# The logits' second product in mixers A and B: 64 rows of the array, or 80 and 128 with zeros added

## The chip, the core and the metric

One core of a Trainium2 chip runs the whole kernel. The metric is the device time of one execution in microseconds (us), the median of three runs; lower is better.

## What is computed

One layer of a decoder over 1024 tokens of 1024 channels, all in float32. The input is normed and projected to the columns of three causal attention mixers and of the merge gates. Each mixer has 8 query heads of 64 channels, with normed queries and keys:

```python
# A: compressed blocks, selected blocks and a 256-key window, two key/value heads, three gated branches
logits = einsum('bgrqd,bgqkd->bgrqk', q, k_selected) * scale + bias;  p = softmax(where(valid, logits, -1e30))
logits = einsum('bgrnqd,bgnkd->bgrnqk', q, k_window) * scale + bias   # window 256
o = gate0 * o_cmp + gate1 * o_slc + gate2 * o_win
# B: window of 128 keys, two key/value heads, a learned sink per head in the softmax
# C: dense causal attention, eight key heads, a cumulative log forget gate added to the logits
x = x + (gates * einsum('btnm,nmd->btnd', branches, w_branch)).sum(2) @ w_out
x = x + conv_ffn(rms_norm(x, norm_ffn))
```

## The kernel before

**Split operands.** TensorE (PE) multiplies float32 data in a reduced form, so each operand is split into a high part and a low remainder, and a product is summed from the three larger partial products. Dense projections do that with three matmuls for each piece of 128 contracted rows (`mm3_steps`, lines 258 to 260, three groups in the trace: high by high, high by low, low by high).

**Logits.** A head has 64 channels, half of the array's 128 rows. `make_k` (line 581) builds from a key head two tiles of 128 rows and 1024 keys: U holds the high part twice, V the low part in rows 0 to 63; rows 64 up are free for extra rows. `make_q` (line 618) builds for 512 queries X, with the high part in rows 0 to 63 and the low part in rows 64 to 127, and where wanted Y, with the high part again and extra rows below. The logits of 128 queries against a bank of up to 512 keys are then two matmuls into one PSUM bank S (function `logits` in `unit`): line 676 multiplies X and U over 128 rows (high by high and low by high in one), and the second product adds high by low:

```python
nc.tensor.matmul(p, z["x"][:, z["qs"]], u[:, ks], start=True, stop=False)                              # 676
if kext is None:
    nc.tensor.matmul(p, z["x"][0:64, z["qs"]], v[0:64, ks], start=False, stop=True)                    # 678
else:
    nc.tensor.matmul(p, z["y"][0:64 + kext, z["qs"]], v[0:64 + kext, ks], start=False, stop=True)      # 680
```

The extra rows carry additive terms: mixer C puts its forget gates into 4 of them (68 rows), and mixer A's selected branch, for the later 512 queries (c = 1), a block pattern in V (a DMA on POOL's queue, line 1219) and the unseen blocks in Y (16 rows, 80 in all). The other logits need no extra rows and use line 678 over 64 rows: all of A's window branch, A's selected branch for the first 512 queries (c = 0), and all of mixer B. These are 64, 32 and 64 matmuls, 160 in all.

**A unit** (`unit`, line 655) is two such lots of logits. DVE adds the bias table and takes the row extreme on S (line 695, or 691 without a table), ACT takes the exponential (704), DVE the reciprocal of the sum (747), and POOL scales the probabilities p in place (753). Later PE transposes p (788), ACT and DVE split the transposes into high and low (795, 796), and PE multiplies them with the split values (811, 812) into O, which ACT and DVE fold (876, 877) and a DMA stores to scratch.

**Order.** Mixers C, A and B run in this order. PE's instructions stand in an order that the program itself writes: `Line.drive` takes steps from three streams (attention units; transposes and value products; the dense projections as filling) by a rough model of the queues. The other engines' queues are put in order by the framework's scheduler. So what PE does next is fixed: when an operand is late, everything behind it on PE waits. Mixer A's outputs are projected in `merge` (line 1340) while mixer B still runs; B's projection, the output projection and the MLP follow behind with nothing but dense matmuls on PE.

Of the kernel before, what the change touches and what calls it, by code (L numbers as in the profile page):

```python
# [37 lines left out]
# column offsets of the input projection  # L38
# [12 lines left out]
def _onehot(dist, valid, relative):  # L51
    """[33, n]: minus the one-hot of the bucket (less that of the last bucket), row 32 marks invalid."""
    n = dist.shape[0]
    oh = np.zeros((N_BUCKETS + 1, n), np.float32)
    cols = np.arange(n)
    b = _bucket(dist)
    oh[b, cols] -= 1.0
    if relative:
        oh[N_BUCKETS - 1, :] += 1.0
    oh[:, ~valid] = 0.0  # L60
    oh[N_BUCKETS, ~valid] = 1.0
    return oh
# [29 lines left out]
class Slots:  # L92
    """When each of n buffers is free, in the order of use; one that is taken counts as never free until it is put."""
# [14 lines left out]
class Line:  # L108
    """A rough model of the engines' queues, to put streams of work into one order of issue for TensorE."""
# [12 lines left out]
    def on(self, eng, ready, dur):  # L122
        """When an operation of an engine ends that takes the first gap in its queue."""
        t = max(ready, self.now) + self.HOP
        q = self.busy[eng]
        while q and q[0][1] < self.now:
            q.pop(0)
        k = 0
        while k < len(q) and q[k][0] < t + dur:
            t = max(t, q[k][1])  # L130
            k += 1
        q.insert(k, (t, t + dur))
        return t + dur

    def later(self, t, act, *args, tag=None):
        """Have act called at time t: a store queued before its data are there would hold up the loads behind it."""
        heapq.heappush(self.due, (t, next(self.count), tag, partial(act, *args)))
# [5 lines left out]
    def room(self, tag, bufs):  # L143
        """Before a tile of these bufs takes the place of one that is still to be stored."""
        while sum(z[2] == tag for z in self.due) >= bufs:
            self.settle(min(z[0] for z in self.due if z[2] == tag))

    def drive(self, *streams):
        """Streams by falling priority: generators that yield a function telling when their next step may issue."""
        at = [next(x, None) for x in streams]  # L150
        while any(at):
            self.settle(self.now)
            times = [NEVER if f is None else f() for f in at]
            if self.due and self.now < self.due[0][0] < min(times):
                self.now = self.due[0][0]
                continue
            k = next((q for q, t in enumerate(times) if t <= self.now), None)
            if k is None:
                k = min(range(len(at)), key=lambda q: times[q])
                assert times[k] < NEVER, "no stream can go on"  # L160
                self.now = times[k]
            at[k] = next(streams[k], None)
            if at[k] is None and k < 2 and not any(at[:2]):
                self.ended()
        self.settle(NEVER)


class Builder:
# [49 lines left out]
    def wload(self, pools, rows, c0, ncol, nk):  # L218
        """rows: DRAM AP [nk*128, cols]; list of (hi, lo) APs [128, ncol], one for each k piece."""
# [29 lines left out]
    def mm3_steps(self, out, pairs, last, there=None):  # L249
        """out += sum of (hi + lo).T @ (hi + lo) less lo.T @ lo, over pairs ((lhi, llo), (rhi, rlo))."""  # L250
# [66 lines left out]
    def rms_cols(self, pool, acc, rstd):  # L317
        """rstd [128, n] per token from acc [128, n * 128], the squares summed over the d tiles."""
# [9 lines left out]
    def bcast_cols(self, pool, col, dst):  # L328
        """dst [128, 512] = col [128, 4] laid along the free dim, on every partition."""
        nc = self.nc  # L330
        p = self.ps("O")
        for q in range(4):
            b = self.t(pool, [P, P], F32, "bc", 2)
            nc.vector.tensor_scalar(b, self.ones, col[:, q:q + 1], None, op0=ALU.mult)
            nc.tensor.matmul(p[:, q * P:(q + 1) * P], b, self.ident, start=True, stop=True)
        nc.scalar.copy(dst, p)

# [1 line left out]
    # chunk: (first column, columns, [(kind, from, to)]); n: normed heads, v: plain, g: branch gates, f: forget gates  # L339
# [12 lines left out]
    def first(self, xp, s0, wp, sp):  # L352
        """x, normed but for the factor of each token, split; beside it two chunks of the projection."""
# [43 lines left out]
    def tok_chunk(self, wp, sp, name, w=None, done=()):  # L397
        """Token-major columns of the projection to DRAM scratch; yields the PE time spent."""
# [57 lines left out]
    def gate_chunks(self, wp, sp, rbc):  # L456
        """tanh of half the merge gates, d-major, to DRAM scratch."""
# [39 lines left out]
    def lo_first(self, w, bs):  # L497
        """Both halves' products with x's low parts, which then are not needed any more."""
# [14 lines left out]
    def forget(self, sp):  # L513
        """Cumulative log forget gate, heads on partitions, split and laid out for the logits."""
        nc = self.nc
        # log_sigmoid(x) = min(x, 0) - log1p(e), e = exp(-|x|); log1p(e) = 2 atanh(e / (2 + e))
# [54 lines left out]
    def load_tok(self, ap_, tag, name, c0, n, t0, nt, bufs):  # L571
        """Columns of the projection, token-major; (tile, when it is there)."""
# [8 lines left out]
    def make_k(self, ap_, src, gcol):  # L581
        """src [128, 8, 64] token-major; U = [k_hi; k_hi], V = [k_lo; extra rows], [128, 1024] each."""
# [3 lines left out]
        v = self.t(ap_, [P, T], F32R, "V", 2)  # L586
        g = self.gain[0:64, gcol:gcol + 1]
# [17 lines left out]
    def make_v(self, ap_, src):  # L605
        """src [128, 8, 64]; VV [128, 8, 128] = [v_hi | v_lo]."""
# [10 lines left out]
    def make_q(self, ap_, qt, pair, gcol, want_y):  # L617
        """qt [128, 4, cols] token-major; X = [q_hi; q_lo], Y = [q_hi; extra rows], [128, 512] for two heads."""
# [11 lines left out]
        for h in range(2):  # L630
# [6 lines left out]
            if want_y:  # L637
                y = self.t(ap_, [P, 512], F32R, "Y", 4)
                nc.gpsimd.tensor_scalar(y[0:64, :], x[0:64, :].bitcast(F32), 1.0, 1.0, op0=ALU.mult, op1=ALU.mult)
# [9 lines left out]
    def unit(self, ap_, head, c_out, two, at, u, v, kext, span, vv, flags, done=None):  # L649
        """two: of each (query tile, x, y, near, first maximum, gate, sink); a query sees span key tiles.  # L650
        near(w): list of (c0, c1, table or None) for the last bank, covering all its columns [0, w)."""
# [19 lines left out]
        def logits(z, n, bank, base):  # L671
# [5 lines left out]
            if kext is None:  # L677
                nc.tensor.matmul(p, z["x"][0:64, z["qs"]], v[0:64, ks], start=False, stop=True)  # L678
# [78 lines left out]
    def pv_jobs(self, ap_, head, c_out, tiles, span, pts, vv, flags, done):  # L757
        """o[:, c_out:c_out + 256] += [v_hi | v_lo].T @ p.T for two lots of 128 queries, of the same query tile or of successive ones."""
# [67 lines left out]
    def t_stream(self, ap_):  # L826
        """Transposes and products with the values, some banks of the first ahead of the second."""
# [44 lines left out]
    def out_bank(self, ap_, o, n, h, t0, heads):  # L872
        """A bank's outputs, of heads from h on and 512 / heads queries from t0 on, to DRAM scratch."""
# [24 lines left out]
    def fox(self, ap_):  # L898
# [23 lines left out]
        def queries(h, c):  # L922
            """Of the heads h and h + 1."""
# [45 lines left out]
    def near_table(self, pool, m):  # L969
        """(tile, when it is there): [128 queries, 8 heads, 256 keys of the same and the previous tile, backwards]."""  # L970
# [7 lines left out]
    def last(tab, h, w):  # L978
        """The table's part for the last w keys."""
# [21 lines left out]
    def windows(self, tp, which):  # L1001
        """The compression windows of both groups, [positions of a pair, pair, 2 * 64 windows], split."""
# [33 lines left out]
    def compress(self, tp, wp, which, bh, bl):  # L1036
# [8 lines left out]
        # tanh form of gelu, twice its value  # L1045
# [93 lines left out]
    def select(self, ap_, e, r):  # L1139
        """BIG at the key blocks that a query does not see, [128, 4, 16]."""  # L1140
        nc = self.nc
        w5 = self.t(ap_, [P, 512], F32, "pcTl", 1)[:, 0:256].rearrange("p (a j) -> p a j", j=16)
        # key blocks 4 j - 1 to 4 j + 3; what stands before a head's first block is a zero (its neighbour's last one is
        # never valid)
# [17 lines left out]
    def cmp_jobs(self, ap_, heads, e, at, pair, g):  # L1162
        """The compressed branch's part of two heads' outputs, in two banks."""
# [35 lines left out]
    def mixer_a(self, ap_, tcm):  # L1199
# [5 lines left out]
        def queries(g, c, pair):  # L1205
            if pair == 0:
                nxt["qt"] = self.load_tok(ap_, "qt", f"aq{g}", 0, 256, c * 4, 4, 1)
            return (yield from self.make_q(ap_, nxt["qt"], pair, 0, c == 1))
# [3 lines left out]
        for g in range(2):  # L1212
# [4 lines left out]
            uw, vw, w_at = yield from self.make_k(ap_, kw, 1)  # L1217
# [6 lines left out]
            for c in range(2):  # L1224
                xy = first
                for pair in range(2):
# [22 lines left out]
                    for tp in range(2):  # L1249
# [25 lines left out]
                        for q in range(2):  # L1275
                            end = None
                            if q == 1:
# [3 lines left out]
                                                 16 if c == 1 else None, NT, vvs, (False, q == 1), done=end)  # L1281
# [3 lines left out]
    def mixer_b(self, ap_):  # L1285
# [5 lines left out]
        def keys(g):  # L1291
            kt = self.load_tok(ap_, "kt", "bkv", g * 64, 64, 0, NT, 2)
            vt = self.load_tok(ap_, "kt", "bkv", P + g * 64, 64, 0, NT, 2)
            u, v, there = yield from self.make_k(ap_, kt, 3)
# [44 lines left out]
    def merge(self, n, first, macc, mp, wps, sp):  # L1339
        """Add a branch's gates times projection to macc; split the sum at the end when mp is given."""  # L1340
# [47 lines left out]
    def out_proj(self, x1, wps, hp_, sp):  # L1388
        """Residual stream after the mixers, and its normed parts, by halves of the tokens."""
# [218 lines left out]
```

## Time and profile before

| | us |
|---|---|
| device time, median of 3 runs (2033.54 to 2034.82) | 2034.41 |
| span of the profiled execution, first to last instruction | 2033.2 |
| PE busy / its weight loads (PEld) | 2005.0 / 1699.0 |
| DVE / ACT / POOL busy | 1184.6 / 817.8 / 419.5 |

The profiled execution's own time is known by its span alone; the median of the runs lies 1.2 us above it, within the spread of the runs. "L678" in a row is line 678 of the kernel. In a list of PE's instructions in order of time the start counts: matmuls are pipelined, so the duration of one reaches into the next, and PE's busy time includes stretches in which the pipeline is not full. The step from one start to the next is what a matmul costs there. PEld is the load of the stationary operand (128 columns) ahead of each matmul, which can run while the matmul before it streams.

### The profile page before, as it was taken

What the parts mean: (1) busy time and instruction counts of PE and PEld (TensorE: products, weight loads), DVE (VectorE), ACT (ScalarE), POOL (GpSimd) and SP (SyncE); (2) the same over time, 40 slices, a digit from 0 to 9 for tenths busy, and PEclk for the clock granted to TensorE, in tenths of its full rate; (3) what the DMA queues carried; (4) which work ended last, traced back from release to release, by engine and by line L of the source; (5) the groups of instructions that cost most, each with busy time, mean ns of one, the idle gap of its engine ahead of it and who ended that gap; (6) DMA issues with size and microseconds to landing.
All of it is one profiled execution on the core that took longest, in us unless ns stands there. A gap on an engine that the chain in (4) does not pass through costs nothing.

```text
span 2033.2 us, 30629 instructions
## 1 busy us (share of the span) xinstructions
PE 2005.0 (99%) x11047; PEld 1699.0 (84%) x11047; DVE 1184.6 (58%) x2571; ACT 817.8 (40%) x1791; POOL 419.5 (21%) x582
## 2 busy tenths in 40 slices
PE   8999999999999999999999999999999999999999
PEld 8999999998788877888777888888888888888887
DVE  6746677766666666666777675564534434445333
ACT  4434566654545545355765233331221211212211
POOL 2224556544312213122121440000000000000000
PEclk9999999999999999999999999999999999999999
DMA  6434232322221221212434644221111120111102
GB/s 200 139 102 130 76 85 81 97 76 65 56 88 47 67 66 59 71 53 83 126 107 132 211 153 135 68 63 52 42 52 42 42 62 26 58 53 52 47 26 83
DMA packets 179562, 166.23 MB, mean 82 GB/s; under 512 B 41569, under 2 KB 157297, under 8 KB 179412
## 3 DMA queue, kind: packets, MB, share of 16 engines
q1 hardware_dynamic: 179348, 164.15, 27.4%
q8 instruction: 87, 1.43, 0.3%
q14 instruction: 63, 0.52, 0.1%
q0 software_dynamic: 64, 0.13, 0.0%
HBM read 126.20 MB, written 38.04 MB: 81 GB/s over the span
## 4 chain that ended last, share of the span: by engine, by line
PE 93%; DVE 3%; DMA 1%; issue 1%; ACT 1%; POOL 1%; SPq 0%; ACTq 0%; DVEq 0%; POOLq 0%
PE D L258 13%; PE D L259 13%; PE D L260 13%; PE S L259 7%; PE S L258 7%; PE S L260 7%; PE T L788 4%; PE T L260 4%; PE T L259 4%; PE T L258 4%; PE S L676 3%; PE O L811 3%; PE O L812 2%; PE S L678 2%; PE S L680 1%
## 5 line engine op out<-in xcount | busy, mean ns | idle before, releaser
L234 ACT CAST whi<-wraw 128x512 fp32r<-128x512 f32 (+2 forms) x308 | 189.4, 621 | 373.1 <-PE S L259 136.6
L235 DVE TENSOR_TENSOR wlo<-wraw,whi 128x512 fp32r<-128x512 f32 (+2 forms) x308 | 227.1, 743 | 98.8 <-ACT whi L234 94.4
L704 ACT ACTIVATE p<-S,mf 128x512 f32<-128x512 f32 (+3 forms) x320 | 174.4, 548 | 115.6 <-DVE mf L695 102.4
L796 DVE TENSOR_TENSOR pTl<-T,pTh 128x512 fp32r<-128x512 f32 (+2 forms) x248 | 151.0, 616 | 89.5 <-ACT pTh L795 87.3
L258 PE MATMUL D<-whi,xh 128*128 128x256 f32 (+2 forms) x680 | 200.5, 295 | 2.6 <-ACT whi L234 2.6
L259 PE MATMUL D<-wlo,xh 128*128 128x256 f32 (+2 forms) x680 | 193.1, 284 | 2.0 <-DVE wlo L235 2.0
L260 PE MATMUL D<-whi,xl 128*128 128x256 f32 (+2 forms) x680 | 192.6, 283 | 0.0
L795 ACT CAST pTh<-T 128x512 fp32r<-128x512 f32 (+2 forms) x248 | 128.3, 532 | 138.3 <-PE T L788 126.6
L259 PE MATMUL D<-xl,whi 128*128 128x512 f32 x464 | 183.2, 395 | 0.0
L753 POOL TENSOR_SCALAR p<-p,den,gates 128x384 f32<-128x384 f32 (+3 forms) x160 | 107.5, 685 | 326.3 <-DVE den L747 183.8
L258 PE MATMUL D<-xh,whi 128*128 128x512 f32 x368 | 155.8, 423 | 0.0
L260 PE MATMUL D<-xh,wlo 128*128 128x512 f32 x368 | 144.9, 394 | 0.0
L258 PE MATMUL S<-xl,whi 128*128 128x512 f32 x352 | 138.4, 394 | 0.0
L260 PE MATMUL S<-xl,wlo 128*128 128x512 f32 x352 | 138.4, 394 | 0.0
L788 PE MATMUL T<-c,p 128*128 128x128 f32 x864 | 130.5, 274 | 5.9 <-POOL p L753 3.7
L258 PEld LDWEIGHTS D<-whi,xh 128*128 128x128 f32 x680 | 129.3, 190 | 6.2 <-ACT whi L234 3.2
L259 PEld LDWEIGHTS D<-wlo,xh 128*128 128x128 f32 x680 | 129.5, 190 | 3.3 <-DVE wlo L235 2.4
L260 PEld LDWEIGHTS D<-whi,xl 128*128 128x128 f32 x680 | 129.1, 190 | 0.0
L811 PE MATMUL O<-pTh,VV 128*128 128x256 f32 x448 | 122.8, 297 | 1.3 <-DVE osum L877 1.3
L258 PE MATMUL D<-xl,whi 128*128 128x512 f32 x304 | 122.6, 403 | 0.0
L753 POOL TENSOR_SCALAR p<-p,den 128x256 f32<-128x256 f32 (+3 forms) x160 | 89.7, 577 | 147.9 <-DVE den L747 94.1
L260 PE MATMUL D<-xl,wlo 128*128 128x512 f32 x304 | 119.8, 394 | 0.0
(323 smaller groups left out, 4896.4 us busy)
## 6 DMA issues: line engine op xcount, KB each, us to landing
wraw<-w_in SPq DMA_DIRECT2D x96, 256.0 KB
s_gate<-stage SPq DMA_DIRECT2D x48, 256.0 KB
stage<-s_gate SPq DMA_DIRECT2D x48, 256.0 KB
wraw<-w_gate SPq DMA_DIRECT2D x44, 256.0 KB
wraw<-w_up SPq DMA_DIRECT2D x44, 256.0 KB
wraw<-w_down SPq DMA_DIRECT2D x44, 256.0 KB
wraw<-w_out SPq DMA_DIRECT2D x32, 256.0 KB
wraw<-w_branch SPq DMA_DIRECT2D x24, 256.0 KB
```

The source lines that it names most:

```text
L234: nc.scalar.copy(hi[:, :m, :ncol], raw[:, :m, :ncol])
L235: nc.vector.tensor_tensor(out=lo[:, :m, :ncol], in0=raw[:, :m, :ncol], in1=hi[:, :m, :ncol].bitcast(F32), op=ALU.subtract)
L258: nc.tensor.matmul(out, lh, rh, start=(k == 0), stop=False)
L259: nc.tensor.matmul(out, lh, rl, start=False, stop=False)
L260: nc.tensor.matmul(out, ll, rh, start=False, stop=(k == n - 1))
L676: nc.tensor.matmul(p, z["x"][:, z["qs"]], u[:, ks], start=True, stop=False)
L704: nc.scalar.activation(pt, z["tiles"][n][:, :w], AF.Exp, bias=z["m"], scale=-1.0, accum_out=den[:, n, q:q + 1])
L753: nc.gpsimd.tensor_scalar(pt, pt, d0[:, q:q + 1], 1.0 if gate is None else gate, op0=ALU.mult, op1=ALU.mult)
L788: nc.tensor.transpose(p[:, c0:c0 + P], z["t"][:, k:k + P], self.ident)
L795: nc.scalar.copy(ph[:, lo:hi], p[:, lo:hi])
L796: nc.vector.tensor_tensor(out=pl[:, lo:hi], in0=p[:, lo:hi], in1=ph[:, lo:hi].bitcast(F32), op=ALU.subtract)
L811: nc.tensor.matmul(ow, vv[:, kj, :], parts["h"][:, cs], start=(b_first and s == 0), stop=False)
```

## The change

The second product is issued over more rows, the added ones zero on one side. Line 678 now reads X and V over all 128 rows; for that `make_k` takes a flag `plain` that sets rows 64 to 127 of V to zero with POOL, used for A's window keys and for B's keys. The selected branch always takes the path of line 680 with 16 extra rows; for c = 0 `make_q` now makes Y too, and sets its 16 extra rows to zero with POOL. Comments and docstrings were removed as well, which shifts later line numbers by up to 5: 676 becomes 681, 678 becomes 683, 680 becomes 685, 639 becomes 644, 753 becomes 758; the new zeroing stands at lines 588 (V) and 643 (Y).

```diff
-    def make_k(self, ap_, src, gcol):
+    def make_k(self, ap_, src, gcol, plain=False):
...
         v = self.t(ap_, [P, T], F32R, "V", 2)
+        if plain:
+            nc.gpsimd.memset(v[64:128, :].bitcast(F32), 0.0)
...
-    def make_q(self, ap_, qt, pair, gcol, want_y):
+    def make_q(self, ap_, qt, pair, gcol, want_y, zeros=0):
...
                 y = self.t(ap_, [P, 512], F32R, "Y", 4)
+                if zeros:
+                    nc.gpsimd.memset(y[64:64 + zeros, :].bitcast(F32), 0.0)
                 nc.gpsimd.tensor_scalar(y[0:64, :], x[0:64, :].bitcast(F32), 1.0, 1.0, op0=ALU.mult, op1=ALU.mult)
...
             if kext is None:
-                nc.tensor.matmul(p, z["x"][0:64, z["qs"]], v[0:64, ks], start=False, stop=True)
+                nc.tensor.matmul(p, z["x"][:, z["qs"]], v[:, ks], start=False, stop=True)
...  mixer_a
-            return (yield from self.make_q(ap_, nxt["qt"], pair, 0, c == 1))
+            return (yield from self.make_q(ap_, nxt["qt"], pair, 0, True, 16 if c == 0 else 0))
...
-            uw, vw, w_at = yield from self.make_k(ap_, kw, 1)
+            uw, vw, w_at = yield from self.make_k(ap_, kw, 1, True)
...
-                                                 16 if c == 1 else None, NT, vvs, (False, q == 1), done=end)
+                                                 16, NT, vvs, (False, q == 1), done=end)
...  mixer_b
-            u, v, there = yield from self.make_k(ap_, kt, 3)
+            u, v, there = yield from self.make_k(ap_, kt, 3, True)
```

On PE no instruction changes its place; 32 second products read Y in place of X, and 128 read more rows. The first window units of mixer A, PE before (S is the logits' bank, D a dense projection that fills in):

```order
L812 MATMUL O_6196<-pTl_6436,VV_5558 128x256
L676 MATMUL S_6475<-U_6194,X_6184 128x256
L678 MATMUL S_6475<-V_6195,X_6184 128x256
L676 MATMUL S_6481<-U_6194,X_6187 128x256
L678 MATMUL S_6481<-V_6195,X_6187 128x256
L676 MATMUL S_6492<-U_6194,X_6184 128x256
L678 MATMUL S_6492<-V_6195,X_6184 128x256
L258 MATMUL D_6400<-whi_6162,xh_37_118 128x256
```

and of the change:

```order
L817 MATMUL O_6203<-pTl_6443,VV_5558 128x256
L681 MATMUL S_6482<-U_6200,X_6184 128x256
L683 MATMUL S_6482<-V_6201,X_6184 128x256
L681 MATMUL S_6488<-U_6200,X_6190 128x256
L683 MATMUL S_6488<-V_6201,X_6190 128x256
L681 MATMUL S_6499<-U_6200,X_6184 128x256
L683 MATMUL S_6499<-V_6201,X_6184 128x256
L258 MATMUL D_6407<-whi_6162,xh_37_118 128x256
```

The rows stand in the same order; only the tiles' numbers differ.

On POOL's queue 20 instructions are new: 4 of line 588, 8 of line 643 and 8 copies into Y (644). The end of mixer C and the start of A, POOL before (p is probabilities to be scaled, the last unit of mixer C; pTh and pTl the split transposes; sqh and rr belong to a projection's norm; blk is the block pattern):

```order
L753 TENSOR_SCALAR p_6036<-p_6036,den_5994 128x512
L753 TENSOR_SCALAR p_6038<-p_6038,den_5994 128x384
L753 TENSOR_SCALAR p_6092<-p_6092,den_5994 128x512
L753 TENSOR_SCALAR p_6094<-p_6094,den_5994 128x512
L428 TENSOR_TENSOR sqh_6145<-stage_6142 128x256
L802 MEMSET pTh_6210 128x128
L803 MEMSET pTl_6211 128x128
L433 TENSOR_TENSOR rr_6147<-rr_6147,mhalf_74 128x4
L599 TENSOR_SCALAR U_6194<-U_6194 64x512
L1219 DMA V_6266<-blk 16x1024
L599 TENSOR_SCALAR U_6194<-U_6194 64x512
```

and of the change:

```order
L1224 DMA V_6273<-blk 16x1024
L643 MEMSET Y_6558 16x512
L758 TENSOR_SCALAR p_6036<-p_6036,den_5994 128x512
L758 TENSOR_SCALAR p_6038<-p_6038,den_5994 128x384
L758 TENSOR_SCALAR p_6092<-p_6092,den_5994 128x512
L758 TENSOR_SCALAR p_6094<-p_6094,den_5994 128x512
L428 TENSOR_TENSOR sqh_6145<-stage_6142 128x256
L807 MEMSET pTh_6217 128x128
L808 MEMSET pTl_6218 128x128
L644 TENSOR_SCALAR Y_6187<-X_6184 64x512
L644 TENSOR_SCALAR Y_6193<-X_6190 64x512
L433 TENSOR_TENSOR rr_6147<-rr_6147,mhalf_74 128x4
```

The DMA of the block pattern and a zeroing of Y moved ahead of the scaling of mixer C's last unit, and two copies into Y stand behind it; the same move of the DMA occurs at the second group of mixer A.

## Rows read from the trace of the kernel before

**Rows 1.** The page: the span, TensorE's busy time with its share of the span and its instructions, and the chain of work that ended last, by engine.

```profile
span 2033.2 us, 30629 instructions
PE 2005.0 (99%) x11047; PEld 1699.0 (84%) x11047; DVE 1184.6 (58%) x2571; ACT 817.8 (40%) x1791; POOL 419.5 (21%) x582
...
PE 93%; DVE 3%; DMA 1%; issue 1%; ACT 1%; POOL 1%; SPq 0%; ACTq 0%; DVEq 0%; POOLq 0%
```

**Rows 2.** Busy time of each engine by stage, core 0: start and end of the stretch in us from the span's start, its length, busy us and number of instructions of PE, PEld, DVE, ACT and POOL, granted TensorE clock, DMA share, GB/s. The stretches are mixer C, mixer A with the start of B, the rest of B, and the projections and the MLP behind it.

```profile
177.00:460.00 283.00, 274.38 (x2184) 268.37 (x2183) 203.20 (x490) 171.49 (x418) 156.21 (x253) 0.99 0.31 84
460.00:980.00 520.00, 517.16 (x2893) 426.20 (x2893) 330.22 (x909) 262.39 (x634) 134.37 (x191) 1.00 0.24 67
980.00:1103.00 123.00, 120.48 (x611) 91.09 (x611) 96.81 (x282) 88.05 (x271) 31.50 (x66) 1.00 0.36 106
1103.00:2033.10 930.10, 926.25 (x4016) 749.76 (x4013) 445.42 (x681) 221.66 (x337) 48.99 (x34) 1.00 0.24 73
```

**Rows 3.** The instructions of line 678: number, duration in ns (least, median, greatest), first and last start in us, shapes; and the idle time of the weight loads just before them (us, times).

```profile
L678 PE MATMUL S<-V,X x160: 379/382/502, 462.6 to 1095.5; 64*128 64x256 f32 x96, 64*128 64x384 f32 x56, 64*128 64x512 f32 x8
...
  issue: 26.8, 105
```

**Rows 4.** PE in order of time at the first units of mixer A: start in us, duration in us, line, operation, tiles, rows*columns of the array in use, moving operand, count.

```profile
462.43 0.28 PE L676 MATMUL S<-U,X 128*128 128x256 f32 x1
462.63 0.38 PE L678 MATMUL S<-V,X 64*128 64x256 f32 x1
462.94 0.39 PE L676 MATMUL S<-U,X 128*128 128x256 f32 x1
463.26 0.38 PE L678 MATMUL S<-V,X 64*128 64x256 f32 x1
463.57 0.39 PE L676 MATMUL S<-U,X 128*128 128x256 f32 x1
463.89 0.38 PE L678 MATMUL S<-V,X 64*128 64x256 f32 x1
464.20 0.39 PE L258 MATMUL D<-whi,xh 128*128 128x256 f32 x1
464.42 0.28 PE L259 MATMUL D<-wlo,xh 128*128 128x256 f32 x1
```

**Rows 5.** PE in order of time where a second product over 80 rows stands next to one over 64; columns as in rows 4.

```profile
660.35 0.28 PE L676 MATMUL S<-U,X 128*128 128x256 f32 x1
660.47 0.29 PE L680 MATMUL S<-V,Y 80*128 80x256 f32 x1
660.59 0.34 PE L676 MATMUL S<-U,X 128*128 128x384 f32 x1
660.86 0.44 PE L678 MATMUL S<-V,X 64*128 64x384 f32 x1
661.24 0.50 PE L258 MATMUL D<-xh,whi 128*128 128x512 f32 x1
661.57 0.39 PE L259 MATMUL D<-xl,whi 128*128 128x512 f32 x1
661.80 0.39 PE L260 MATMUL D<-xh,wlo 128*128 128x512 f32 x1
```

**Rows 6.** PE in order of time: a pair of 384 columns with 80 rows, and two groups of four transposes: the first behind a product over 128 rows, the second behind one of line 678.

```profile
593.57 0.34 PE L676 MATMUL S<-U,X 128*128 128x384 f32 x1
593.75 0.34 PE L680 MATMUL S<-V,Y 80*128 80x384 f32 x1
...
1076.77 0.60 PE L788 MATMUL T<-c,p 128*128 128x128 f32 x4
...
1079.05 0.66 PE L788 MATMUL T<-c,p 128*128 128x128 f32 x4
```

**Rows 7.** PEld, the weight loads, in order of time at the place of rows 4; columns as there.

```profile
462.63 0.18 PEld L678 LDWEIGHTS S<-V,X 64*128 64x128 f32 x1
462.94 0.19 PEld L676 LDWEIGHTS S<-U,X 128*128 128x128 f32 x1
...
464.31 0.19 PEld L259 LDWEIGHTS D<-wlo,xh 128*128 128x128 f32 x1
```

**Rows 8.** Busy time of each engine, columns as in rows 2, in the 20 us in which DVE is busiest in the rest of mixer B.

```profile
1000.00:1020.00 20.00, 19.04 (x98) 14.11 (x98) 19.22 (x59) 18.49 (x57) 5.26 (x10) 1.00 0.45 134
```

**Rows 9.** What PE waited for in mixer C, 177 to 460 us: us in total, times, longest us (gaps over 0.15 us).

```profile
PE T L788 <- POOL p L753: 2.4, 1, 2.4
PE D L259 <- DVE wlo L235: 2.0, 2, 1.6
PE T L788 <- POOL Y L639: 1.0, 1, 1.0
```

**Rows 10.** POOL's instructions by line and shape: count, busy us, mean ns of one, idle us before them and what ended it.

```profile
L428 POOL TENSOR_TENSOR sqh<-stage 128x512 f32<-128x512 f32 x32 | 35.5, 1111 | 96.6 <-ACT stage L422 95.7 <-DVE rr L431 0.9
L639 POOL TENSOR_SCALAR Y<-X 64x512 fp32r<-64x512 f32 x24 | 15.2, 632 | 16.2 <-ACT X L633 16.2
L802 POOL MEMSET pTh<- 128x128 f32 x32 | 6.6, 205 | 27.9 <-PE O L811 25.0 <-PE O L812 2.7
```

**Rows 11.** POOL's DMA of the block pattern into rows 64 to 79 of V, first group of mixer A: duration in ns, start in us.

```profile
L1219 POOL DMA_DIRECT2D V<-blk x1: 727/727/727, 447.4 to 447.4; - x1
```


## The prediction

> **What bounds the kernel now.** First the page: PE holds 93% of the chain that ended last and counts as busy for 99% of a span of 2033.2 us [rows 1]. The reader should see two things: time taken off PE is nearly time off the kernel, and busy time cannot say what there is to take, since a matmul's duration covers its waiting in the pipeline too. Second, the stages [rows 2]: DVE, ACT and POOL stay below PE in all of them, but DVE is busy for 203.20 of 283 us in mixer C (72%), for 330.22 of 520 in mixer A (64%) and for 96.81 of 123 in mixer B (79%). In the last 930 us there is no attention; the change does not reach them. Third, line 678 by itself: 160 matmuls, all between 462.6 and 1095.5 us, their least duration 379 ns for moving operands of only 256 columns, and 26.8 us of idle weight loads just before them, in 105 gaps, for which the profile names no releaser [rows 3]. An engine that stops with nothing to wait for is the mark to look for. Last, PE in order of time, to read what one such matmul costs from start to start.
>
> **The cost of a second product over 64 rows.** For 256 columns the usual step is 0.12 us: 660.35 to 660.47 to 660.59, the middle one a second product over 80 rows of line 680 [rows 5]. Around line 678 [rows 4] the step into it is 0.20 to 0.32, the step out of it 0.31, and the one after that, 464.20 to 464.42, still 0.22. From 462.43 to 464.42 seven steps take 1.99 us where 7 x 0.12 = 0.84 would do; 1.15 over three products is 0.38 each. The width does not matter: with 384 columns the step into line 678 is 0.27, out 0.38, then 0.33 before a 512-column matmul [rows 5], against 0.18 for 384 columns with 80 rows [rows 6] and 0.23 for 512 (661.57 to 661.80) [rows 5]: 0.09 + 0.20 + 0.10 = 0.39. In front of transposes the last part is smaller: four of them take 0.66 us behind line 678 and 0.60 otherwise [rows 6], so 0.09 + 0.20 + 0.06 = 0.35. Along PE's order 25 of the 160 stand ahead of transposes, 135 do not. I read it as PE changing between a part of the array and all of it, emptying itself both ways, with the next load exposed: line 678's load starts with its matmul (462.63 in both lists), so does the load of the matmul behind it (462.94), while 464.31 is ahead of its matmul at 464.42 [rows 4, 7].
>
> The Trainium skill, TensorE: Matmul & The Clock Gate, Part 2 (step 4, drain), puts the emptying of the array at about 128 cycles. The granted clock is 1.00 in both mixers, the 2.4 GHz level [rows 2], so that is an estimate of 53 ns; two per product and 160 products give 17 us by the page, against the 60 us that the next part adds up from rows. The measurement decides.
>
> **What the change takes from PE.** All 160 become products over 80 or 128 rows in the same places. Line 680 with 80 rows stands at full pace in rows 5 and 6, line 676 with 128 rows likewise (660.47 follows 660.35 by 0.12), so nothing of the cost should be left: 135 x 0.38 + 25 x 0.35 = 60 us. The bounds of this term are 160 x 0.09 = 14 us, the entry steps alone, if the others were caused by something else, and 160 x 0.39 = 62. I take 60, because the exits are seen behind line 678 alone and are gone behind line 680 next to it.
>
> **What it adds.** On PE no instruction. On POOL 20: 8 copies into Y at 632 ns; 8 zeroings of 512 columns and 4 of 1024. The nearest row, a zeroing of 128 columns, has 205 ns; by columns that is 0.82 and 1.64 us, together 5.1 + 6.6 + 6.6 = 18 us [rows 10]. As a floor each zeroing costs 0.2 us (in all 8 us), as a ceiling what a product of two 512-column operands does, 1.11 us, and twice that for 1024 (in all 23) [rows 10]. POOL is busy for 166 of the 643 us of mixers A and B [rows 2], so its idle time covers them; without that cover they would cost these 18 us. The order of the queue is the open side: behind the zeroings and the moved DMA of the block pattern stand the scalings of p, for which PE's transposes wait. Their operands (old V and Y tiles) were last read by logits of the unit that is scaled next, or older ones, and a scaling needs the sums over those same logits, which come later. So the added waits end before the wait behind them; I price them at nothing, at most at a gap like PE's single one of 2.4 us on p in mixer C [rows 9]. The DMA takes POOL 0.73 us and is issued at 447.4 us today [rows 11]; it moves ahead, while its first reader, a selected unit of c = 0, comes behind the window units that start at 462.4 us [rows 4]. The copies into Y for c = 0 are new operands, made as for c = 1 today, and PE waited for such a copy once, 1.0 us [rows 9].
>
> **What is late next.** Mixers A and B hold 96 and 64 of the products, 36 and 24 us of the 60. In A, 520 - 36 = 484 us remain and DVE's share goes from 64% to 68%. PE's idle time is 2.8 us of 520 there at 64% and 8.6 of 283 in mixer C at 72% (length less busy time) [rows 2]; halfway, 1.8% of 484 is 8.7, so some 6 us come back; the gaps of C are partly weights and start-up [rows 9], so I take 4, with 0 and 12 (all of C's rate) as bounds. In B, 123 - 24 = 99 us would remain for PE and DVE has 96.8 us of work. The best that DVE reaches there is 19.22 of 20 us [rows 8]; over a whole stretch with its chains of bank, row extreme, exponential and transposes I take 90%, 96.8 / 0.9 = 107.6 us. So B gets back 15 of its 24 us, with 22 (at 96%) and 0 (DVE and ACT as today) as bounds. **Sum:** 60 - 4 - 9 = 47; 2033.2 - 47 = 1986 of span. The median lies 1.2 us above that execution's span, so 2034.4 - 47 = **1987 us**.
>
> **Rivals.** *All of it arrives:* DVE, ACT and POOL hold back no more than today, 2034.4 - 60 = 1974. For it: PE's idle time in A is only 2.8 us, and DVE does run at 96% at the worst place. Against it: in B, 99 us of PE against 96.8 of DVE. *DVE takes over:* B gains nothing since its chain is then DVE and ACT throughout, and A falls to C's rate of waiting: 36 - 12 = 24, so 2010. For it: from 1000 to 1020 us DVE and ACT are at 19.22 and 18.49 of 20 already [rows 8]. Against: that is one slice, with the splits of A's outputs crowded into it. *No gain:* the steps out of line 678 belong to loads that cannot run ahead of a matmul in the same rows of the array, and the new products inherit them; PE saves nothing and the time stays at 2034. Rows 4, 5 and 7 speak against it: loads of all 128 rows run 0.11 us ahead. The Trainium skill, TensorE: Matmul & The Clock Gate, Part 3 (the mechanism), says that a load overlaps running matmuls only when the row group differs; by that sentence this rival would hold, and the trace disagrees. *Slower:* POOL's queue holds p back. A zeroing waits for the last reader of an old V or Y while scalings that PE needs soon stand behind it. To lose, the 20 added instructions have to cost PE over 60 us, 3 us each at all 20 places, more than the longest wait for p of 2.4 us [rows 9]; at 4.5 us each, 90 us, the time would be 2034 - 60 + 90 = 2064.
>
> **How the numbers follow.** Forecast (most of A's part, two thirds of B's, 1979 to 1996) 0.54; all of it 0.24; DVE takes over 0.16; no gain 0.03; slower 0.03. The range runs from 1972, the first rival at 62 us, to 2004, which takes in the nearer half of the DVE rival and leaves out about 0.15. A measurement of this kernel can tell about 0.2%, 4 us, from no change. Faster by more than that: the first three cases, 0.94; same 0.03; slower 0.03.
>
> **What would show it.** In the profile after: lines 683 and 685 at steps of 0.12, 0.18 and 0.23 us by width, loads ahead of their matmuls, and no idle loads without a releaser; the stretch of mixer A about 32 us shorter and that of B about 15; mixer C and the 930 us behind B unchanged within 2 us; DVE near 90% in B, and PE's new gaps there named after DVE or ACT (pTl, the exponential). Steps that stay at 0.3 us behind line 683 would break the first term; a stretch of B that stays at 123 us would break the second; PE waiting for p in many places would break the price of POOL.

## The result, and the profile after

| us | before | after |
|---|---|---|
| device time, median (range; 4 runs each on one chip) | 2034.62 (2033.54 to 2037.2) | 1984.27 (1983.81 to 1984.62) |
| span of the profiled execution | 2033.2 | 1982.0 |

The ratio is 0.9753, with a 95% interval of 0.9739 to 0.9767: 50.35 us less, where 47 was forecast. The page of the changed kernel answers to [rows 1]:

```profile
span 1982.0 us, 30637 instructions
...
PE 1948.7 (98%) x11047; PEld 1695.1 (86%) x11047; DVE 1178.1 (59%) x2571; ACT 814.7 (41%) x1791; POOL 433.7 (22%) x602
...
PE 92%; DVE 3%; ACT 1%; DMA 1%; issue 1%; POOL 0%; SPq 0%; DVEq 0%; ACTq 0%; POOLq 0%
```

PE still holds the chain, with 56 us less busy time for the same 11047 instructions; DVE has 3% of the chain, as before. By stages, cut at the same places of the program as [rows 2] (mixer C, A, B; start and length, then busy time of each engine, granted clock, DMA share, GB/s):

```profile
176.00:459.00 283.00, 274.60 (x2186) 268.77 (x2186) 202.62 (x491) 171.64 (x418) 161.13 (x261) 0.99 0.31 84
459.00:943.00 484.00, 479.83 (x2891) 424.12 (x2890) 327.42 (x907) 259.91 (x630) 144.17 (x204) 1.00 0.25 72
943.00:1051.50 108.50, 101.77 (x612) 89.02 (x611) 94.27 (x284) 86.77 (x274) 32.15 (x66) 0.97 0.42 122
```

Mixer C keeps its 283 us, A goes from 520 to 484, B from 123 to 108.5, and what follows stays at 930. In B, DVE is now busy for 94.27 of 108.5 us (87%), and PE is idle for 6.7 us there (2.5 before).

The second products by line (count, duration in ns least/median/most, first and last start, shapes), to be read against [rows 3]:

```profile
L683 PEld LDWEIGHTS S<-V,X x128: 187/188/333, 461.0 to 1043.5; 128*128 128x128 f32 x128
L683 PE MATMUL S<-V,X x128: 274/283/415, 461.1 to 1043.6; 128*128 128x256 f32 x80, 128*128 128x384 f32 x48
...
L685 PE MATMUL S<-V,Y x192: 280/340/495, 176.6 to 915.1; 68*128 68x512 f32 x40, 80*128 80x512 f32 x40, 68*128 68x256 f32 x32, 80*128 80x256 f32 x32
```

The least duration fell from 379 to 274 ns, and no idle time stands before line 683's matmuls or loads any more. PE and its loads in order of time at the place of [rows 4] and [rows 7]:

```profile
461.14 0.27 PE L683 MATMUL S<-V,X 128*128 128x256 f32 x1
461.25 0.28 PE L681 MATMUL S<-U,X 128*128 128x256 f32 x1
461.37 0.28 PE L683 MATMUL S<-V,X 128*128 128x256 f32 x1
461.49 0.28 PE L681 MATMUL S<-U,X 128*128 128x256 f32 x1
461.61 0.28 PE L683 MATMUL S<-V,X 128*128 128x256 f32 x1
461.73 0.28 PE L258 MATMUL D<-whi,xh 128*128 128x256 f32 x1
```

```profile
461.03 0.19 PEld L683 LDWEIGHTS S<-V,X 128*128 128x128 f32 x1
461.14 0.19 PEld L681 LDWEIGHTS S<-U,X 128*128 128x128 f32 x1
```

Every step is 0.11 to 0.12 us, and each load starts 0.11 us ahead of its matmul.

**Times by PE's own order.** All kernels of this study but e5 and e6 issue PE's instructions in the same order, so the time between the starts of the same two can be compared from profile to profile, free of how long the kernel took to start. (PE's 1380th instruction, 3.7 us into mixer C's stretch, started between 179.3 and 183.3 us in kernels that do not differ up to there: this scatter is in every total.) Four pieces are used below: A's piece, PE's instructions 3575 to 6390 (93 second products); B's head, 6390 to 6450 (6); the **crowded stretch**, 6450 to 6700 (28); and B's rest, 6700 to 7040 (30). The crowded stretch runs from 947.49 to 996.23 us in the changed kernel. In us:

| kernel | A's piece | B's head | crowded | B's rest |
|---|---|---|---|---|
| before | 505.53 | 14.13 | 51.92 | 66.20 |
| e3 zeros only | 505.55 | 14.13 | 51.59 | 66.20 |
| e1 A only | 472.05 | 14.13 | 51.58 | 66.20 |
| e2 B only | 505.53 | 11.83 | 48.54 | 56.10 |
| after | 472.05 | 11.83 | 48.74 | 56.09 |
| e10 after again | 472.10 | 11.83 | 48.54 | 56.09 |
| e4 A's outputs unsplit | 472.05 | 11.83 | 48.62 | 56.08 |
| e7 C's outputs unsplit | 472.07 | 11.83 | 45.65 | 56.70 |
| e11 C's weights unsplit | 473.65 | 11.83 | 47.00 | 55.70 |
| e12 both unsplit | 472.04 | 11.83 | 43.04 | 55.73 |
| e8 subtractions on POOL | 472.05 | 11.83 | 49.68 | 56.38 |
| e9 both on POOL | 472.03 | 11.83 | 50.00 | 56.18 |

Each row is one profiled execution. A's piece repeats within 0.1 us in all kernels but e11, where the granted clock fell (last section); the crowded stretch repeats within 0.2 us in the four kernels with the same work there (e2, after, e10, e4) and within 0.4 in before, e3 and e1. So a microsecond can be placed. At 0.378 us for each product (the prediction's 0.38, with 0.35 in front of transposes, would give at most 0.2 less in a piece) the four pieces would save 35.2, 2.3, 10.6 and 11.3; they saved 33.5, 2.3, 3.2 and 10.1. **Of the 10 us that are missing, 7.4 are missing in the crowded stretch.**

### The profile page after: what moved, and what is told of

It is laid out like the page before. It is cut to its first block, busy times and chain, and to the rows that moved or that the text cites. A ratio compares the mean times of both kernels' runs of the same rounds, so it can differ in the third digit from the quotient of the medians.

```text
span 1982.0 us, 30637 instructions
## 1 busy us (share of the span) xinstructions
PE 1948.7 (98%) x11047; PEld 1695.1 (86%) x11047; DVE 1178.1 (59%) x2571; ACT 814.7 (41%) x1791; POOL 433.7 (22%) x602
## 4 chain that ended last, share of the span: by engine, by line
PE 92%; DVE 3%; ACT 1%; DMA 1%; issue 1%; POOL 0%; SPq 0%; DVEq 0%; ACTq 0%; POOLq 0%
PE D L259 13%; PE D L258 13%; PE D L260 13%; PE S L259 7%; PE S L260 7%; PE S L258 7%; PE T L793 4%; PE T L259 4%; PE T L260 4%; PE T L258 4%; PE O L817 3%; PE O L816 2%; PE S L681 2%; PE S L685 2%; PE S L683 1%
## 5 line engine op out<-in xcount | busy, mean ns | idle before, releaser
L817 PE MATMUL O<-pTl,VV 128*128 128x256 f32 x448 | 117.2, 285 | 2.1 <-DVE pTl L801 2.1
```

What stands on the lines that cost most here:

```text
L817: nc.tensor.matmul(ow, vv[:, kj, :], parts["l"][:, cs], start=False, stop=(b_last and s == len(bank) - 1))
```

## The experiments

### e1 and e2: each mixer alone

```diff
 # e1: B's units go back to 64 rows (kext 0)
+            elif kext == 0:
+                nc.tensor.matmul(p, z["x"][0:64, z["qs"]], v[0:64, ks], start=False, stop=True)
-            u, v, there = yield from self.make_k(ap_, kt, 3, True)
+            u, v, there = yield from self.make_k(ap_, kt, 3)
...
 # e2: A's window and c = 0 units go back, likewise
-            uw, vw, w_at = yield from self.make_k(ap_, kw, 1, True)
+            uw, vw, w_at = yield from self.make_k(ap_, kw, 1)
```

> The change in mixer A alone: its 96 second products over 80 or 128 rows, mixer B's 64 left over 64 rows. PE's order is the same; 16 of POOL's 20 new operations and the 2 zeroings of A's V stay, B's 2 are gone. Theory (A's products sit where PE alone is the bound, so nearly all of 36 us arrives): 35 us saved, 1999 to 2001 us, and the stretch of B as long as before (123 us). Rival (POOL's additions or DVE eat into A as forecast, 4 us): 2002 to 2004.

> The change in mixer B alone: 64 second products over 128 rows, A's 96 left over 64. Theory (PE has 24 us less, DVE and ACT hold back 9 of them, all in B): 15 us saved, 2018 to 2021 us, and with the run of A alone the two savings add up to that of the whole change, 50 us. Rival (the loss of 9 us comes from A having become faster, so that its outputs and B's start crowd together): with A as slow as before, B alone saves 20 us or more, 2011 to 2015.

Measured: e1 1999.07 us (ratio to before 0.9834, 0.9819 to 0.9848), e2 2017.73 (0.9924, 0.9910 to 0.9939), so 35.6 and 16.9 us less than before on their chip, 52.5 together against 50.35 for the whole: the same, by totals that scatter by some microseconds. e1 lies in the range of its theory, and e2, 0.3 us below that of its own, is outside its rival's. By PE's order the two parts add up, within 0.4 us in every piece: e1 has A's piece of after and B's of before, e2 the other way round. B gives back its third with or without A's part, so the loss belongs to B itself.

### e3: the zeros without the rows

```diff
-                    ... max(k_at, xy[0][2], tb_at), u, v, None, 2, vv,
+                    ... max(k_at, xy[0][2], tb_at), u, v, 0, 2, vv,
 # the same for A's window (None to 0) and A's selected branch, c = 0 (16 to 0): POOL's work stays, PE reads 64 rows
```

> All of POOL's additions (8 copies into Y, 8 zeroings of Y, 4 of V, the DMA of the block pattern moved ahead), but all 160 second products over 64 rows as before, so that nothing is gained. Theory (POOL's idle time covers them): 2033 to 2036 us, within 1.5 us of before. Rival (they hold back the scaling of p, and a part of the 10 us that did not arrive is theirs): 2038 us or more.

Measured: 2035.8 us, ratio 1.0006 (0.9997 to 1.0015). POOL's added work costs nothing that the times show, though its queue does stand still for it. In the changed kernel, by line (POOLq is POOL's own queue of waits):

```profile
L643 POOL MEMSET Y<- x8: 518/520/523, 385.4 to 675.7; 16x512 f32 x8
L643 POOLq EVENT_SEMAPHORE  x6: 17/301/1497, 384.1 to 668.5; - x6
...
L588 POOLq EVENT_SEMAPHORE  x4: 17/17/7540, 405.2 to 908.0; - x4
L588 POOL MEMSET V<- x4: 947/952/957, 405.7 to 915.6; 64x1024 f32 x4
```

The zeroings take 4.2 and 3.8 us where 6.6 and 6.6 had been estimated, and one waited for its V tile for 7.5 us with POOL's queue behind it. PE's one wait for p in A is 1.7 us, against 1.3 before.

### e5 and e6: is it the 64 rows, or the change to and from them?

Both are the kernel before with 64 rows; a unit takes its two banks S at once and issues its four products in one of two orders.

```diff
+        elif kext is None:
+            yield lambda: max(self.s_s.free[1] if len(self.s_s.free) > 1 else NEVER, self.s_p.peek(), at)
...
+            for q, part in ((0, 0), (0, 1), (1, 0), (1, 1)):      # e5: first, second, first, second
+            for q, part in ((0, 0), (1, 0), (0, 1), (1, 1)):      # e6: first, first, second, second
+                second(lots[q], part)
```

> The kernel before, with the logits of a unit's two lots issued in one go where the second product has 64 rows: both banks are taken first, then the order is first product, second product, first, second. Control for the next run: same waits, same places, 160 second products over 64 rows, each between products over 128 rows. Both theories: 2025 to 2045 us (two banks taken at once cost some waiting), with steps of 0.32 us around line 678 as before.

> As the control, but within a unit the order is first, first, second, second: the 64-row products stand in 80 groups of two. Theory (the cost belongs to the change between 64 and 128 rows, one way and back): the second of a group follows the first by 0.12 us (256 columns), 0.18 (384), half of the changes are gone, 80 x 0.38 = 30 us less on PE and 22 to 30 us less than the control. Rival (each 64-row product costs 0.38 us by itself): the second of a group again takes 0.3 us, and the time is that of the control within 2 us.

Measured: e5 2061.69 us (ratio 1.0131, 1.0114 to 1.0149), e6 2034.1 (0.9996, 0.9986 to 1.0005): with the second products side by side 27.6 us less, 0.34 for each of the 80 pairs. The expectation for the control e5 was missed: taking two banks at once made the program write another order for PE from the start of mixer A on, and e5 took 27 us more than before; what in that order costs them was not followed up. Between e5 and e6 only the two products in the middle of each of the 80 pairs change places. PE in order of time, one unit, e5 first and then e6:

```profile
462.45 0.28 PE L691 MATMUL S<-U,X 128*128 128x256 f32 x1
462.66 0.38 PE L694 MATMUL S<-V,X 64*128 64x256 f32 x1
462.97 0.39 PE L691 MATMUL S<-U,X 128*128 128x256 f32 x1
463.28 0.38 PE L694 MATMUL S<-V,X 64*128 64x256 f32 x1
463.59 0.39 PE L258 MATMUL D<-whi,xh 128*128 128x256 f32 x1
463.81 0.28 PE L259 MATMUL D<-wlo,xh 128*128 128x256 f32 x1
```

```profile
461.41 0.39 PE L691 MATMUL S<-U,X 128*128 128x256 f32 x2
461.73 0.50 PE L694 MATMUL S<-V,X 64*128 64x256 f32 x2
462.16 0.39 PE L258 MATMUL D<-whi,xh 128*128 128x256 f32 x1
462.38 0.28 PE L259 MATMUL D<-wlo,xh 128*128 128x256 f32 x1
```

From the first S product to the second D matmul e5 takes 1.36 us and e6 0.97, for the same five steps: 0.39 less, one change there and back. Two products over 64 rows in a row pay once. So the cost belongs to the change between 64 rows and 128, not to a 64-row matmul as such. One part of the expectation failed: by the starts of the single instructions, the second product of a group follows the first not by 0.12 and 0.18 us but by 0.22 and 0.28 (medians at 256 and 384 columns), and the step out of the group is 0.21 and 0.27 where e5 has 0.31 and 0.37. So each change, in or out, costs 0.09 us at once and 0.10 at the step behind it; the prediction's 0.20 for the step out of a single product is the end of one change and the beginning of the next.

### e4 and e7: what crowds the stretch at 960 us

The idle time of PE in B, after, by what it waited for:

```profile
PE S L681 <- ACT p L709: 3.2, 3, 1.4
PE O L817 <- DVE pTl L801: 1.7, 2, 1.4
PE T L793 <- DVE pTl L801: 1.0, 1, 1.0
PE T L793 <- DVE X L637: 0.4, 1, 0.4
```

PE waits for ACT's exponential and DVE's transposed low parts. Two windows of 10 us in the middle of it, DVE (third) and ACT (fourth) without any room:

```profile
960.00:970.00 10.00, 8.52 (x52) 7.09 (x51) 9.87 (x31) 9.90 (x33) 4.14 (x6) 1.00 0.30 96
970.00:980.00 10.00, 7.34 (x48) 6.30 (x47) 9.82 (x31) 9.61 (x30) 1.85 (x5) 0.91 0.69 189
```

Into this stretch fall the splits for a projection in `merge`, of outputs (line 1360 on ACT, 1361 on DVE):

```profile
L1360 ACT CAST xl<-xl x8: 603/616/621, 954.9 to 964.4; 128x512 fp32r<-128x512 f32 x8
...
L1361 DVE TENSOR_TENSOR xl<-xl x8: 672/687/694, 955.5 to 965.6; 128x512 fp32r<-128x512 f32 x8
```

The question is whether these hold B back, or B's own attention chain does. e4 meant to leave them out:

```diff
+                if n == 0:                       # e7: n == 2
+                    parts[h][k] = (ol, ol)
+                else:
+                    nc.scalar.copy(oh, raw)
+                    nc.vector.tensor_tensor(out=ol, in0=raw, in1=oh.bitcast(F32), op=ALU.subtract)
```

> The changed kernel, and in the projection of mixer A's outputs the split of these outputs into high and low is left out (8 casts on ACT of 0.6 us and 8 subtractions on DVE of 0.65 us; the matmuls read the loaded tiles for both parts, so this branch's values are wrong); PE's order is the same. These 16 operations run from 954 to 966 us in the changed kernel, where PE lost most. Theory (what B did not get back is lost where the splits crowd DVE and ACT): about 7 us less than the changed kernel, 1976 to 1979 us, and PE idle in that stretch 1 us or less. Rival (B's own chain of DVE and ACT is the bound over all of B): 1 to 2 us less, 1982 to 1984.

Measured: 1982.0 us, ratio 0.9742 (0.9726 to 0.9759), the crowded stretch 48.62. **e4 was aimed at the wrong operations.** The instructions that vanished lay behind 1051.5 us: the program projects mixer C's outputs first, during B, and A's only after B. What falls at 955 to 966 us are the splits of C's outputs; the sentences above on A's outputs, in the section on the kernel, in the rivals and in this expectation, are wrong in that. e4 says nothing on either theory; it shows only that A's splits cost nothing. e7 is the same edit for C's.

> The changed kernel without the split of mixer C's outputs into high and low parts (the eight casts on ACT and eight subtractions on DVE that fall at 954 to 966 us, inside mixer B; both operands then read the loaded tile, so C's part of the output is wrong by a factor). Left out: 8 casts of 616 ns and 8 subtractions of 687 ns, nothing on PE. Theory (B gives back its 9 us because these 16 operations fall into the one stretch where DVE and ACT have no room, and TensorE's granted clock falls to 0.75 in the slice after the idle): 1976 to 1980 us, the stretch 960 to 980 us has PE busy over 19 of 20 us and the granted clock stays at 1.00 through B. Rival (B's own attention chain on DVE and ACT sets its pace once PE is faster, whatever else is there): 1982 to 1984.5 us.

Measured: 1982.9 us, ratio 0.9742 (0.9726 to 0.9758), the changed kernel again on the same chip (e10) 1982.85. By the total the rival would win; but the profiled execution of e7 started its attention 3.6 us later than after did, which is within the scatter of the start and larger than the effect that is looked for. By PE's order the crowded stretch fell from 48.7 to 45.65 us: 3.0 of the missing 7.4, a part of what the theory wanted; B's rest grew by 0.6. The totals show nothing of these 2.4 us and, with starts that scatter by 4 us, cannot decide. Two of the theory's other signs failed: from 960 to 980 us PE was busy for 17.75 us, not 19, and the clock still fell, to 0.91 from 980 to 1000 us.

### e8 and e9: the same work on POOL

```diff
-                nc.vector.tensor_tensor(out=ol, in0=raw, in1=oh.bitcast(F32), op=ALU.subtract)
+                (nc.gpsimd if n == 2 else nc.vector).tensor_tensor(out=ol, in0=raw, in1=oh.bitcast(F32), op=ALU.subtract)
 # e9: the cast for n == 2 as well: nc.gpsimd.tensor_copy(out=oh, in_=raw)
```

> The changed kernel with the eight subtractions of mixer C's split on POOL instead of DVE, all of the computation kept. DVE is relieved of 5.5 us at 955 to 966 us, ACT is not; POOL gets eight operations of about 1.1 us (128x512 multiplications of two operands take 1127 ns on it) where it is busy 6 of 20 us. Theory (no room on DVE and ACT there): 1979 to 1983 us, a part of what leaving out the split gives, with ACT as what PE waits for. Rival (the splits don't matter): 1983.5 to 1985 us. Second rival (POOL's normalisations of p come late behind these): over 1985 us.

> As the run before, with the eight casts of mixer C's split on POOL too: ACT is relieved of 4.9 us as well, and POOL gets 16 operations, some 16 us in a stretch of 20 us where it has 14 free. Theory (no room on DVE and ACT): 1977 to 1981 us, close to the kernel without the split. Rival (the splits don't matter): 1983.5 to 1985 us. Second rival (POOL's normalisations of p queue behind these and hold up the transposes): 1985 to 1992 us.

> The changed kernel itself, unedited, on the chip of the three runs above, as what they are measured against: both theories expect 1984 to 1985 us.

Measured: e8 1984.4 us (ratio 0.9753, 0.9736 to 0.9770), e9 1985.61 (0.9758, 0.9741 to 0.9774), e10 1982.85 (0.9743, 0.9727 to 0.9759). Neither gains, and e10 lies 1.2 us below what was expected of it; the crowded stretch is 49.7 and 50.0 us, a microsecond more than after. By its total e8 falls to the rival "the splits don't matter". But PE waits there for DVE's transposed low parts, not for ACT as had been expected, and the longest of these waits ends at 976.30 us, with two subtractions of weights (line 235, 1.46 us) ahead in DVE's queue:

```profile
PE T L793 <- DVE pTl L801: 3.9, 2, 2.8
```

In e9, POOL's subtraction takes 1.28 us where DVE's took 0.69, with the scalings of p queued between; PE's longest wait in the stretch, from the waits, and then POOL in order of time just ahead of its end:

```profile
PE T L793 <- POOL p L758: 4.2, 1, 4.2
```

```profile
969.91 2.53 POOL L1364 TENSOR_TENSOR xl<-xl 128x512 fp32r<-128x512 f32 x2
972.42 1.14 POOL L758 TENSOR_SCALAR p<-p,den 128x128 f32<-128x128 f32 x2
973.54 1.26 POOL L1364 TENSOR_TENSOR xl<-xl 128x512 fp32r<-128x512 f32 x1
974.78 1.36 POOL L758 TENSOR_SCALAR p<-p,den 128x256 f32<-128x256 f32 x2
```

The second rival of e9 held: p comes late. In both, moving the work moved the wait.

### e11 and e12: the rest of the projection's splits

Besides C's outputs, the weights of C's projection are split at 970 to 976 us and later. POOL now copies them once, and both operands read the copy.

```diff
+            if getattr(self, "bare", False):      # set for n == 2 alone
+                nc.gpsimd.tensor_copy(out=hi[:, :m, :ncol], in_=raw[:, :m, :ncol])
+                lo = hi
 # e12: and the edit of e7
```

> The changed kernel with the weights of mixer C's projection (w_branch of mixer C) not split: POOL copies the loaded weights into the tile that both operands read; ACT's eight casts (620 ns) and DVE's eight subtractions (684 ns) for them are left out, so C's part of the output is wrong by a factor. Measured between the same two instructions of PE, from B's product that stands at 947.5 us in the changed kernel to the transpose at 996.2 us there: before 51.9 us, the changed kernel 48.7 and 48.5 (two runs), without the split of C's outputs 45.7; if all that the 28 products of the stretch save arrived, 51.9 - 28 x 0.378 = 41.3 us. Theory (any work of the projection on DVE and ACT that falls at 950 to 990 us is paid by PE): 45 to 47.5 us. Rival (B's own softmax and transposed copies alone): 48.3 to 48.9 us.

> The same, and the split of mixer C's outputs left out too (as two runs earlier): none of the splitting for C's projection is left on DVE and ACT, and C's part of the output is wrong by a factor. Same stretch of PE. Theory (the projection's splits on DVE and ACT are what B gives back there): 41.3 to 43.5 us, and about 1978 to 1981 us in all. Rival (B's own softmax and transposed copies set the rest): 45 to 46 us, as without the split of the outputs alone.

Measured: e11 1982.79 us (ratio 0.9749, 0.9734 to 0.9763), e12 1978.99 (0.9731, 0.9715 to 0.9748); the crowded stretch 47.0 and 43.0 us, both in the range of the theory and outside that of the rival. Against the mean of after and e10, 48.6, that is 1.6 and 3.0 (e7) for the parts apart and 5.6 together, a microsecond more than their sum. (e12's total, too, is in the range expected, but the intervals of its ratio and of after's overlap.) With both gone, no wait for the exponential is listed for PE any more; all its waits from 943 to 1000 us, and one window (compare DVE's 19.69 and ACT's 19.51 us in the two windows above):

```profile
PE T L797 <- DVE pTl L805: 1.0, 1, 1.0
PE O L820 <- DVE osum L886: 1.0, 1, 1.0
PE O L821 <- DVE pTl L805: 0.6, 1, 0.6
PE T L600 <- DVE pTl L805: 0.2, 1, 0.2
```

```profile
960.00:980.00 20.00, 18.01 (x117) 15.61 (x117) 16.80 (x59) 17.42 (x57) 8.69 (x18) 1.00 0.58 179
```

The projection's transfers are all still there (the DMA engines' share is 0.58 in this window), so they alone are not what held PE up. One reservation: leaving these splits out of the kernel before was not tried. It could have gained there too, at most about what PE idled in B, 2.5 us [rows 2], nearly all of it in the crowded stretch (51.93 us, 49.54 of them busy on PE; the view of before):

```profile
985.84:1037.77 51.93, 49.54 (x252) 36.63 (x251) 43.97 (x131) 42.02 (x127) 15.73 (x32) 1.00 0.43 130
```

So, by this estimate, between 3 and 5.6 us of what B gave back are the splits'.

## Why the prediction was right, step by step

- **The price of a product over 64 rows: right.** 0.38 us each; A's piece and B's head, where little else interferes, gave 33.5 / 93 = 0.36 and 2.3 / 6 = 0.38. e6 adds what the prediction had only read from rows: it is the change of rows that is paid, there and back, 0.19 us each way. The estimate by the drain that the Trainium skill gives (TensorE: Matmul & The Clock Gate, Part 2), 17 us for all 160, is a third of the 50 that arrived.
- **No gain, since loads wait in the same rows: refuted.** The loads of line 683 run 0.11 us ahead of their matmuls while a matmul over the same 128 rows is running. So the sentence of the Trainium skill (TensorE: Matmul & The Clock Gate, Part 3, The mechanism), that a load overlaps running matmuls only where the row group differs, does not hold in this trace; what the same section says of loads into the background weight buffer would fit.
- **What POOL adds, priced at nothing: right,** by e3, with 13 us of work (5.0, 4.2 and 3.8) where 18 had been estimated.
- **A gives back 4: too much.** 35.2 - 33.5 = 1.7 us over 93 products. A's rate of idle time moved less towards C's than taken, and the rival in which DVE takes over (12 us back in A, all 24 in B) is refuted by the same pieces.
- **B gives back 9: right in size (24.2 - 15.6 = 8.6), half right in its mechanism,** so that the size is in part luck. The step took DVE at 90% over the whole of B, by its total of work. DVE reached 87%, but the loss is not spread: B's head lost nothing, its rest 1.2 us, the crowded stretch 7.4. There the splits for C's projection meet B's softmax on DVE and ACT, with DVE at 19.69 and ACT at 19.51 of 20 us; e12 gets back 5.6 of the 7.4 by taking those splits away (of which up to 2.5 might have been had before the change too). The prediction had seen that place in the kernel before [rows 8] and named the splits, as A's, but used the row only as a best rate. About 2 us remain that no run explains further; by the waits of e12 they are B's own chain on DVE.
- **Sum:** 47 forecast, 50.35 measured; A's 2.3 us are most of the difference, 0.4 come from B, and the last 0.6 us is less than the totals can tell.

## What to carry to other kernels

A matmul over 64 rows between matmuls over 128 costs its change there and back, here 0.38 us whatever its width (256 to 512 columns); filling the unused rows with zeros on one side removes it, putting two such matmuls side by side halves it, and the zeros are cheap on an engine with idle time. When PE gets faster, look at which 20 us of the stage DVE and ACT are full, not at their mean over it: most of what B lost was lost in that place. Before work is moved off a full engine, see what is queued behind it on the new one: POOL had the time and still held p back.

## What the runs showed of the hardware beside that

In the changed kernel the granted clock was 0.91 from 970 to 980 us and 0.75 from 980 to 990, behind 10 us in which PE had been busy for 7.34; four transposes took 1.05 us at 980.00, against 0.60 in e10 at 980.19. The window and the four transposes, first of the changed kernel, then of e10:

```profile
980.00:990.00 10.00, 10.00 (x53) 9.16 (x53) 8.06 (x21) 7.01 (x20) 4.74 (x10) 0.75 0.42 124
```

```profile
980.00 1.05 PE L793 MATMUL T<-c,p 128*128 128x128 f32 x4
```

```profile
980.00:990.00 10.00, 8.75 (x57) 7.52 (x57) 8.72 (x26) 7.54 (x20) 4.91 (x10) 1.00 0.46 141
```

```profile
980.19 0.60 PE L793 MATMUL T<-c,p 128*128 128x128 f32 x4
```

The steps between matmuls of 256 columns were 0.21 us there, against 0.12: the 1.2 GHz level. In e10, the same kernel, the clock stayed at 1.00 and PE waited for DVE instead, and the stretch took 48.54 us against 48.74. So the lower clock cost next to nothing there: it took time that PE would have waited anyway. In e7, e8 and e9 it fell too. Where little else holds PE up it is not free: in e11 the granted clock was 0.86 from 700 to 710 us, inside A, against 1.00 in e12 (PE busy for 7.89 us in both), and around there e11 lost the 1.6 us by which its A piece is longer. What made the clock fall at 970 us in one execution of the changed kernel and not in the other, with PE's idle time nearly the same ahead of it (2.66 and 2.65 us from 970 to 980), stays open.
